# The opening of an encoder layer on one core: modulation columns on VectorE, low weight parts by DMA, x on two queues

## The chip, the core and the metric

The kernel runs as one program on one core of a Trainium2 chip. The core has five engines with an instruction queue each: TensorE (PE, matrix products; its weight loads are listed apart as PEld), VectorE (DVE), ScalarE (ACT), GpSimd (POOL) and SyncE (SP), which here only issues transfers. An engine works through its queue in order, and an instruction that has to wait holds up those behind it. Transfers between main memory and the on-chip memory are issued from SP's, ACT's or POOL's queue and are carried by 16 DMA engines that all queues share. The metric is the device time of one execution in microseconds.

## The reference

One encoder layer on a sequence of 512 tokens with 1024 channels, batch 1, all in float32. A conditioning vector c gives nine modulation vectors of 1024 numbers: shift, scale and gate for each of three sub-layers. The sub-layers are a SwiGLU feed-forward network, a mixer of two kinds of attention, and a second SwiGLU network.

```python
c_act = jax.nn.silu(c)
mod = c_act @ w_mod[l] + b_mod[l]
(sh1, sc1, g1, sh2, sc2, g2, sh3, sc3, g3) = jnp.split(mod, N_MOD, axis=-1)
h = modulate(rmsnorm(x, norm_ffn1[l]), sh1, sc1)          # h * (1 + scale) + shift
x = x + 0.5 * g1[:, None, :] * swiglu(h, w_ffn1_in[l], w_ffn1_out[l])
```

The change is about the first two and the fourth of these lines and about the first products of the fifth. What follows (the mixer, the second network) is not touched.

## The kernel before

**Layout.** Everything is kept transposed: channels lie on the 128 partitions, in eight chunks (`NC` = 8) of 128 channels, and the 512 tokens lie along the free axis. A column is 128 numbers, one per partition: for one modulation vector there are eight columns, one for each chunk. `par` holds small parameters as columns: the three norm gains, the 72 bias columns of `b_mod`, and one more.

**Split products.** A float32 product is made of three products in a faster format: a tensor is split into a high part (a rounding copy) and a low part (what the rounding left), and high times high, high times low and low times high are added up. `split_from` (lines 158 to 160) does that with a copy on ScalarE (line 159) and a subtraction on VectorE (line 160). `load_main`, used later in the kernel, does it in another way (lines 601 to 603): ScalarE writes the high part and also its negative, and a transfer from POOL's queue adds the weights from main memory onto the negative, which leaves the low part.

**A modulation column.** `mod_load` asks for a 128 x 1024 block of `w_mod` on SP's queue (line 196). `mod_col` multiplies it by the broadcast Silu of c (`cact`) and sums each row in one instruction on VectorE (line 206), then adds the bias and puts in the rest with one or two instructions on a single column (lines 213 to 219). For the shift columns of the opening GpSimd makes the product (line 453) and ScalarE the row sum (line 204).

**The opening** (lines 431 to 485). The order of TensorE, VectorE and ScalarE is written out by hand there. SP and GpSimd are ordered by a planner that goes by modelled times, as all engines are in most of the kernel's stages unless a `manual_schedule` block names them.

1. c is broadcast over the partitions by TensorE (line 434). x comes in eight transfers on SP's queue, with `par` after the second (lines 189 and 191).
2. ScalarE squares each chunk of x (line 438), VectorE adds the squares up (line 440), TensorE sums them over the partitions (line 277), VectorE adds the epsilon (line 247), GpSimd takes the power -1/2 (line 248). VectorE puts the result on a diagonal (line 256), and TensorE spreads it over all partitions (line 269).
3. For each chunk k, `hidden` makes the modulated, normalised input: VectorE scales x (line 286, here called the scale step), ScalarE adds the shift and rounds (line 287), VectorE takes the low part (line 289).
4. The first three pairs of column blocks of the network's input weights are multiplied chunk by chunk (line 482): six accumulators, three products each, so 18 products per chunk, with h of that chunk and the block `w1s[k]` of 128 x 768 weights (loaded on line 450, split by `first_split`).

The columns and weights for chunk k + 1 are made while TensorE works on chunk k. The six accumulators take six of the eight banks of the product memory.

**After the opening** `ffn` goes through the other pairs, eight chunks each. After each pair `side1` makes about two more modulation columns (56 are left) and, at its first call, asks for three small inputs (`row`, `pos`, `freq`) that are used much later. Tensors of the kind `u4` (six buffers) hold the `w_mod` blocks, `raw` (four) the weights as loaded, `hi` and `lo` (five each) the split weights; a transfer into a buffer waits on its queue until the last reader of the former content is through.

## Time and profile before

| | |
|---|---|
| time, median of 3 runs | 1116.46 us (1116.37 to 1117.34) |
| the profiled execution's own time | 1117.23 us |
| its span in the trace | 1115.4 us |
| TensorE busy | 1086.0 us (97%) |
| VectorE busy | 739.6 us (66%) |
| ScalarE busy | 536.0 us (48%) |
| GpSimd busy | 147.4 us (13%) |
| first product of the opening / first product after it | 23.47 / 64.50 us |

The span runs from the first to the last instruction of the profiled execution; its own time is 1.83 us longer. A row of the timeline gives the start in us, the duration in us, the engine, the line of the kernel, the operation, what it writes and reads with the shapes, the number of instructions merged in the row, and in brackets the idle time before it with what ended it. [...] Rows of the grouped views give total busy us and mean ns of one.

### The profile page before, as it was taken

To read this page: it belongs to the slowest core of one execution; us is meant where nothing else is said; L and a number is where in the kernel's file an instruction comes from. 1 tells how busy PE (TensorE), PEld (TensorE's weight loads), DVE (VectorE), ACT (ScalarE), POOL (GpSimd) and SP (SyncE) were. 2 spreads that over 40 slices of the span, in tenths; PEclk is the share of its full clock that TensorE was granted. 3 is DMA by queue.
4 is the path that set the end of the run, shared out by engine and by line. 5 is a ranking of instruction groups with operands and counts; after the bars stand their busy time and mean duration, and the time that the engine had idled before them with its cause. 6 is when DMAs were issued, how large, how long until landed. Compare 5 with 4: busy or idle time off the path is not lost.

```text
span 1115.4 us, 16981 instructions
## 1 busy us (share of the span) xinstructions
PE 1086.0 (97%) x6540; PEld 950.5 (85%) x6540; DVE 739.6 (66%) x1441; ACT 536.0 (48%) x895; POOL 147.4 (13%) x152
## 2 busy tenths in 40 slices
PE   4899999999999999999999999999999999999998
PEld 2688888888888998876788877979999999999998
DVE  6998456765733450567642678855888777776767
ACT  3453221223223274567765655534766545654553
POOL 3300000000000011430113300101121111111210
PEclk9999999999999999999999999999999999999999
DMA  8797446766434439874468831862488999799874
GB/s 304 239 353 249 137 153 218 249 242 224 156 87 127 161 115 271 189 171 95 105 158 199 228 103 34 308 187 58 95 200 202 222 231 195 182 224 212 188 145 118
DMA packets 63570, 204.54 MB, mean 183 GB/s; under 512 B 7553, under 2 KB 9729, under 8 KB 63490
## 3 DMA queue, kind: packets, MB, share of 16 engines
q1 hardware_dynamic: 45792, 144.73, 37.6%
q0 software_dynamic: 15392, 54.53, 27.1%
q10 hardware_dynamic: 2306, 4.20, 1.0%
q8 instruction: 51, 0.84, 0.3%
q14 instruction: 29, 0.24, 0.1%
HBM read 194.52 MB, written 8.91 MB: 182 GB/s over the span
## 4 chain that ended last, share of the span: by engine, by line
PE 78%; issue 9%; DVE 5%; DMA 3%; ACT 2%; POOL 1%; SPq 0%; DVEq 0%; POOLq 0%; ACTq 0%
PE sc L154 9%; PE sc L156 9%; PE sc L155 9%; PE acc L154 7%; PE acc L155 6%; PE acc L156 6%; PE sc L1098 3%; PE sc L1100 3%; PE sc L1099 3%; PE acc L1099 3%; PE acc L1100 3%; PE acc L1098 3%; PE acc L656 2%; PE acc L657 2%; PE acc L658 2%
## 5 line engine op out<-in xcount | busy, mean ns | idle before, releaser
L159 ACT CAST hi<-raw 128x1024 fp32r<-128x1024 f32 (+2 forms) x160 | 155.3, 975 | 218.5 <-PE sc L155 130.9
L160 DVE TENSOR_TENSOR lo<-raw,hi 128x1024 fp32r<-128x1024 f32 (+2 forms) x160 | 179.9, 1129 | 60.6 <-ACT hi L159 58.4
L154 PE MATMUL sc<-b,hi 128*128 128x512 f32 (+1 forms) x430 | 159.9, 372 | 0.4 <-ACT b L159 0.4
L155 PE MATMUL sc<-b,hi 128*128 128x512 f32 (+1 forms) x430 | 159.3, 371 | 0.0
L156 PE MATMUL sc<-b,lo 128*128 128x512 f32 (+1 forms) x430 | 159.2, 370 | 0.0
L154 PE MATMUL acc<-b,hi 128*128 128x512 f32 (+1 forms) x352 | 134.1, 381 | 0.0
L155 PE MATMUL acc<-b,hi 128*128 128x512 f32 (+1 forms) x352 | 130.8, 372 | 0.0
L156 PE MATMUL acc<-b,lo 128*128 128x512 f32 (+1 forms) x352 | 130.7, 371 | 0.0
L1098 PE MATMUL acc<-b,hi 128*128 128x256 f32 x374 | 106.2, 284 | 0.1
L1099 PE MATMUL acc<-b,hi 128*128 128x256 f32 x374 | 105.9, 283 | 0.1
L1100 PE MATMUL acc<-b,lo 128*128 128x256 f32 x374 | 105.9, 283 | 0.0
L1100 PE MATMUL sc<-b,lo 128*128 128x256 f32 x358 | 101.4, 283 | 0.0
L1098 PE MATMUL sc<-b,hi 128*128 128x256 f32 x358 | 101.3, 283 | 0.0
L1099 PE MATMUL sc<-b,hi 128*128 128x256 f32 x358 | 101.3, 283 | 0.0
L154 PEld LDWEIGHTS sc<-b,hi 128*128 128x128 f32 x430 | 81.0, 188 | 14.7 <-ACT b L159 0.9
L155 PEld LDWEIGHTS sc<-b,hi 128*128 128x128 f32 x430 | 81.0, 188 | 14.2 <-DVE b L160 0.3
L156 PEld LDWEIGHTS sc<-b,lo 128*128 128x128 f32 x430 | 81.0, 188 | 13.7
L206 DVE CUSTOM_DVE_ANT_0 u<-u,ka 128x1024 f32<-128x1024 f32 x65 | 82.5, 1281 | 12.9 <-DMA u<-w_mod 12.8
L159 ACT CAST hi<-u 128x1024 fp32r<-128x1024 f32 (+1 forms) x51 | 52.2, 1024 | 69.1 <-PE acc L1099 14.1
L160 DVE TENSOR_TENSOR lo<-u,hi 128x1024 fp32r<-128x1024 f32 (+1 forms) x51 | 60.8, 1192 | 28.8 <-ACT hi L159 28.4
L154 PEld LDWEIGHTS acc<-b,hi 128*128 128x128 f32 x352 | 66.4, 189 | 13.7 <-issue 3.5
L156 PEld LDWEIGHTS acc<-b,lo 128*128 128x128 f32 x352 | 66.3, 188 | 11.3
(339 smaller groups left out, 2461.1 us busy)
## 6 DMA issues: line engine op xcount, KB each, us to landing
u<-w_mod SPq DMA_DIRECT2D x72, 512.0 KB, 5.3
raw<-w1i SPq DMA_DIRECT2D x38, 512.0 KB, 4.3
u<-w2i POOLq DMA_DIRECT2D x31, 512.0 KB, 6.1
raw<-w2i SPq DMA_DIRECT2D x31, 512.0 KB, 4.4
raw<-w_gate SPq DMA_DIRECT2D x16, 512.0 KB, 5.1
lo<-w_gate POOLq DMA_DIRECT2D x13, 512.0 KB, 7.3
u<-w2i SPq DMA_DIRECT2D x13, 512.0 KB, 6.9
raw<-w1o SPq DMA_DIRECT2D x16, 384.0 KB, 3.1
```

Source lines behind the costliest of these rows:

```text
L154: PE.matmul(out, wh, xh, start=first, stop=False)
L155: PE.matmul(out, wh, xl, start=False, stop=False)
L156: PE.matmul(out, wl, xh, start=False, stop=last)
L159: S.copy(hi, src)
L160: V.tensor_tensor(lo, src, f(hi), ALU.subtract)
L206: V.tensor_tensor_reduce(out=w, in0=w, in1=cact, scale=1.0, scalar=0.0, op0=ALU.mult, op1=ALU.add, accum_out=t)
L656: PE.matmul(out[t][:, 0:n], hh[k][:, ht], wh[:, o : o + n], start=k == 0, stop=False)
L657: PE.matmul(out[t][:, 0:n], hh[k][:, ht], wl[:, o : o + n], start=False, stop=False)
L658: PE.matmul(out[t][:, 0:n], hl[k][:, ht], wh[:, o : o + n], start=False, stop=k == NC - 1)
L1098: PE.matmul(out, wh[:, s], xh, start=first and j == 0, stop=False, skip_group_check=True)
L1099: PE.matmul(out, wh[:, s], xl, start=False, stop=False, skip_group_check=True)
L1100: PE.matmul(out, wl[:, s], xh, start=False, stop=last and j == 1, skip_group_check=True)
```

## The change

- The columns: the bias, and for gates the factor, is the start value of the reduction, so that a shift or gate column is one instruction. `mod_begin` prepares such start values for all eight columns of a vector at once. A scale column is the reduction and one more instruction. All of them, the shift columns of the opening too, are made on VectorE; GpSimd's product and ScalarE's row sum are gone.
- The weights of the opening: for chunks 1, 3, 5 and 7 the low part is made in `load_main`'s way (two passes on ScalarE and an adding transfer from POOL's queue); for the even ones VectorE subtracts as before, in `first_low`. The high parts are made one chunk earlier than before, and the loads of three chunks are asked for at the start.
- x: chunks 6 and 7 are asked for on POOL's queue, the others on SP's; `par` goes to ACT's queue.
- The norm: the sums are made with `Norm.add` and `close`, in two groups (the sum of seven squares, and the last square). The two Silus of c come after the fourth square.
- TensorE multiplies the identity by itself, 8 + 5 + 4 times, between the steps ahead of the first product.
- The three products of a chunk come in the order high-high, high-low(h), low(weights)-high.
- The order of SP and POOL in the opening is now written out by hand as well.
- The three small inputs are asked for when fewer than 52 columns are left.

```diff
-        nc.sync.dma_start(x[c], a["x"][c])
-        if c == 1:
-            nc.sync.dma_start(par, a["par"])
+        (G if c in BY_POOL else nc.sync).dma_start(x[c], a["x"][c])
...
+    def mod_begin(v):
+        if v in (SH1, SH2, SH3):
+            return par[:, BMOD + v * NC : BMOD + (v + 1) * NC]
...
+        t, begin = modv[v][:, c : c + 1], mod_begin(v)[:, c : c + 1]
+        by = 1.0 if v in norms or v in (SH1, SH2, SH3) else -0.5 if v == G3 and c % 4 < 2 else 0.5
+        V.tensor_tensor_reduce(
+            out=w, in0=w, in1=cact, scale=by, scalar=0.0 if v in norms else begin, op0=ALU.mult, op1=ALU.add,
+            accum_out=t,
+        )
+        if v in norms:
+            V.scalar_tensor_tensor(t, t, par[:, norms[v] + c : norms[v] + c + 1], begin, ALU.mult, ALU.add)
...
-    with tc.manual_schedule(engines={mybir.EngineType.DVE, mybir.EngineType.Activation, mybir.EngineType.PE}):
+    with tc.manual_schedule(engines=BOUND | {mybir.EngineType.SP, mybir.EngineType.Pool}):
...
+        def warm(n):
+            out = bank("sc")[:, 0:P]
+            for i in range(n):
+                PE.matmul(out, ident, ident, start=True, stop=True)
+        warm(8)
+        def first_loads(k):
+            scale = mod_load(SC1, k)
+            raw = sbuf("raw", [P, 1024], F32, RAW)
+            nc.sync.dma_start(raw[:, 0:768], a["w1s"][k])
+            w1[k] = scale, mod_load(SH1, k), raw
+        def first_split(k):
...
+            S.copy(hi, raw)
+            if k in BY_DMA:
+                S.activation(lo, raw, AF.Identity, scale=-1.0)
+                G.dma_start(lo, a["w1s"][k], accum_op=ALU.add)
+        def first_low(k):
+            raw, hi, lo = w1[k][2:]
+            if k not in BY_DMA:
+                V.tensor_tensor(lo, raw[:, 0:768], f(hi), ALU.subtract)
+        for k in range(3):
+            first_loads(k)
+        mod_begin(SC1)
         n1 = Norm()
         for c in range(NC):
+            n1.add(c)
+            if c == 3:
+                for i in range(2):
+                    S.activation(cact[:, i * T : (i + 1) * T], cb[i], AF.Silu)
+        rs = n1.close()
         mod_col(SC1, 0, w1[0][0])
+        warm(5)
+        diag = n1.diagonal(rs)
+        rb1 = n1.spread(diag)
+        warm(4)
         mod_col(SH1, 0, w1[0][1])
+        out1 = [b for _ in range(3) for b in pair_banks()]
         first_split(0)
         for k in range(NC):
             h1 = hidden(rb1, k, SC1, SH1, hh[k], hl[k])
             next(h1)
+            if k + 3 < NC:
+                first_loads(k + 3)
             if k == 0:
+                first_split(1)
+                first_low(0)
+            elif k + 1 < NC:
+                mod_col(SC1, k + 1, w1[k + 1][0])
+            next(h1)
+            if k == 0:
+                mod_col(SC1, 1, w1[1][0])
+            wh, wl = w1.pop(k)[3:]
+            for w, h in ((wh, hh[k]), (wh, hl[k]), (wl, hh[k])):
...
             if k + 1 < NC:
+                mod_col(SH1, k + 1, w1[k + 1][1])
+                first_low(k + 1)
+            if k + 2 < NC:
+                first_split(k + 2)
...
-        while small_loads:
+        credit[0] += n
+        while small_loads and len(rest) < 52:
             nc.sync.dma_start(*small_loads.pop())
-        credit[0] += n
```

More of the change, by code (lines that the diff above doesn't have):

```diff
@@ L435, in layer @@
+        for k in range(3):
+            first_loads(k)
+        mod_begin(SC1)
         n1 = Norm()
         for c in range(NC):
-            sq = f2()
-            S.activation(sq, x[c], AF.Square)
-            if c:
-                V.tensor_tensor(sq, sq, before, ALU.add)
-            before = sq
-        n1.sums(sq, FULL[0], True, True)
-        for i in range(2):
-            S.activation(cact[:, i * T : (i + 1) * T], cb[i], AF.Silu)
-        w1 = {}
-        def first_loads(k):
-            w1[k] = [mod_load(v, k) for v in ((SH1, SC1) if k else (SC1, SH1))]
-            raw = sbuf("raw", [P, 1024], F32, RAW)
-            nc.sync.dma_start(raw[:, 0:768], a["w1s"][k])
-            w1[k].append(raw)
-            if k:
-                G.tensor_tensor(w1[k][0], w1[k][0], cact, ALU.mult)
-                mod_col(SC1, k, w1[k][1])
@@ L470, in layer @@
             next(h1)
+            if k + 3 < NC:
+                first_loads(k + 3)
             if k == 0:
[L472 to L479 removed]
+                first_split(1)
[7 more added lines that the diff above has]
+            for w, h in ((wh, hh[k]), (wh, hl[k]), (wl, hh[k])):
                 for i, out in enumerate(out1):
[L481 to L482 removed]
+                    first, last = k == 0 and w is wh and h is hh[k], k == NC - 1 and w is wl
+                    PE.matmul(out, w[:, i * P : (i + 1) * P], h, start=first, stop=last)
             if k + 1 < NC:
[L484 to L485 removed]
+                mod_col(SH1, k + 1, w1[k + 1][1])
+                first_low(k + 1)
+            if k + 2 < NC:
+                first_split(k + 2)
     rest = [(v, c) for v in (G1, SC2, SH2, G2, SC3, SH3, G3) for c in range(NC)]
```

59 lines of the change are left out of this document (21 added, 38 removed).

## The prediction

> **What bounds the kernel now.** I read the head of the page first, then the busy time by stages (columns: stretch, its length, busy time of PE, PEld, DVE, ACT and POOL, granted clock, DMA share, GB/s).
>
> ```profile
> span 1115.4 us, 16981 instructions
> 24.00:65.00 41.00, 36.86 (x147) 27.47 (x146) 39.56 (x65) 20.16 (x33) 10.64 (x5) 1.00 0.74 255
> 65.00:200.00 135.00, 135.00 (x597) 111.84 (x596) 89.41 (x157) 38.44 (x51) 0.00 (x0) 1.00 0.62 213
> ```
>
> From 65 us on TensorE has no idle time (135.00 of 135), so what ends before 65 us shifts the rest. In the opening the full engine is VectorE: 39.56 of 41 us. Next the timeline of TensorE: the first row is the first product of the opening, then come the first products of chunks 6 and 7 and the first one after the opening.
>
> ```profile
> 23.47 0.80 PE L482 MATMUL acc<-b,hi 128*128 128x512 f32 x1 [3.56 <-ACT b L287]
> 56.17 0.44 PE L482 MATMUL acc<-b,hi 128*128 128x512 f32 x1
> 60.31 0.48 PE L482 MATMUL acc<-b,hi 128*128 128x512 f32 x1
> 64.50 0.39 PE L154 MATMUL acc<-b,hi 128*128 128x512 f32 x1
> ```
>
> The opening's products run from 23.47 to 64.50 us. A chunk with nothing missing takes 60.31 - 56.17 = 4.14 or 64.50 - 60.31 = 4.19, so 4.15 us for 18 products. Eight would be 33.2 us; they take 41.0. The timeline of VectorE, with GpSimd's row beside it, shows chunk 4, one period of it:
>
> ```profile
> 38.67 0.74 DVE L286 SCALAR_TENSOR_TENSOR f<-x,mod,op 128x512 f32<-128x512 f32 x1
> 39.33 1.22 DVE L206 CUSTOM_DVE_ANT_0 u<-u,ka 128x1024 f32<-128x1024 f32 x1
> 40.47 0.08 DVE L206 DVE_READ_ACCUMULATOR2_ANT mod<- 128x1 f32 x1
> 40.53 2.40 POOL L453 TENSOR_TENSOR u<-u,ka 128x1024 f32<-128x1024 f32 x1 [4.91 <-DMA u<-w_mod]
> 40.59 0.22 DVE L213 TENSOR_SCALAR mod<-mod,par 128x1 f32<-128x1 f32 x1
> 40.84 2.10 DVE L214 TENSOR_TENSOR mod<-mod,par 128x1 f32<-128x1 f32 x1
> 42.86 0.74 DVE L289 SCALAR_TENSOR_TENSOR b<-f,mod,b 128x512 fp32r<-128x512 f32 x1
> 43.53 0.15 DVE L216 TENSOR_TENSOR mod<-mod,par 128x1 f32<-128x1 f32 x1
> 43.60 0.95 DVE L160 TENSOR_TENSOR lo<-raw,hi 128x768 fp32r<-128x768 f32 x1
> 44.46 0.73 DVE L286 SCALAR_TENSOR_TENSOR f<-x,mod,op 128x512 f32<-128x512 f32 x1
> ```
>
> From scale step to scale step 44.46 - 38.67 = 5.79 us, of which a one-column multiply takes 2.10: it ends at 42.94, just as GpSimd's two-input multiply does (40.53 + 2.40 = 42.93). VectorE is held while GpSimd multiplies. The same holds in the head, where the chain to the first product reads:
>
> ```profile
> 2.94 3.75 PE L434 MATMUL sc<-u,ones 1*128 1x512 f32 x4 [2.94 <-DMA u<-c]
> 8.57 1.97 ACT L438 ACTIVATE f<-x 128x512 f32<-128x512 f32 x3 [0.29 <-DMA x<-x]
> 10.45 1.06 ACT L444 ACTIVATE ka<-sc 128x512 f32<-128x512 f32 x2
> 5.26 0.68 DVE L440 TENSOR_TENSOR f<-f,f 128x512 f32<-128x512 f32 x1
> 11.68 1.87 PE L277 MATMUL tp<-ones,f 128*128 128x2 f32 x8 [4.99 <-DVE f L440]
> 13.59 0.16 DVE L247 TENSOR_SCALAR sm<-tp 128x4 f32<-128x4 f32 x1 [0.37 <-PE tp L277]
> 13.84 1.03 POOL L248 TENSOR_TENSOR sm<-sm,half 128x4 f32<-128x4 f32 x1 [12.52 <-DVE sm L247]
> 14.90 2.34 POOL L453 TENSOR_TENSOR u<-u,ka 128x1024 f32<-128x1024 f32 x1
> 14.90 2.88 DVE L256 TENSOR_TENSOR f<-ident,sm 128x512 f32<-128x512 f32 x1 [1.15 <-POOL sm L248]
> 17.84 2.08 PE L269 MATMUL op<-f,ones 128*128 128x512 f32 x2 [4.29 <-DVE f L256]
> 18.96 2.17 DVE L216 TENSOR_TENSOR mod<-mod,par 128x1 f32<-128x1 f32 x1
> 21.92 0.74 DVE L286 SCALAR_TENSOR_TENSOR f<-x,mod,op 128x512 f32<-128x512 f32 x1
> ```
>
> The diagonal (2.88) sits under such a multiply too, and a one-column add takes 2.17 where chunk 4's takes 0.15. I call the start of the first scale step t0 (21.92 here); the first product follows 23.47 - 21.92 = 1.55 us later.
>
> **The change, the loop.** GpSimd's seven multiplies and ScalarE's row sums go; VectorE does the shift columns itself. Its price by the period above, start to start: scale step 39.33 - 38.67 = 0.66. A column with its reduction 40.47 - 39.33 = 1.14, as a shift column now ends, so 1.15. A scale column needs the total back and one more small step: 40.59 - 39.33 = 1.26 to the first small step and about 0.11 for it, 1.37; today it is two steps. The low part of h 43.53 - 42.86 = 0.67, taken as 0.66. The low part of a weight chunk 44.46 - 43.60 = 0.86, taken as 0.87, now for even chunks only. A start value read from a column in the reduction is in no row; I take 0 and allow 0.1 us each, 1.6 in all; a gain is excluded, since nothing is taken out of the reduction.
>
> So a chunk with no low part next costs 0.66 + 1.37 + 0.66 + 1.15 = 3.84, with one 4.71. Chunks 0, 1, 3, 5 carry one: the scale steps start at t0 + 0, 4.71, 9.42, 13.26, 17.97, 21.81, 26.52, 30.36. A chunk's products start 1.55 later or 4.15 after the former chunk's: t0 + 1.55, 6.26, 10.97, 15.12, 19.52, 23.67, 28.07, 32.22. The opening ends at t0 + 36.4. TensorE alone would give 1.55 + 33.2 = 34.8: the two engines are nearly level, so either alone can lose 1.5 us unseen. The low part of h now comes behind the scale column, at 0.66 + 1.37 + 0.74 + 0.1 = 2.87 after the scale step; its products are second now, 1.55 + 6 x 0.23 = 2.93 after it: just covered.
>
> ScalarE in its longest chunk has one high part of h and two passes over a weight chunk, about 0.72 + 2 x 0.82 = 2.4 of 4.3 us, and waits there for a weight chunk loaded three chunks ahead. Behind that wait stands the next high part of h, for which TensorE waits; the loads are asked for as their buffers are given back, over two periods (8.6 us) ahead of use, against these times to landing (queue rows of the DMA view, the last line for the accumulating loads; then the rates by queue and one stretch of the head):
>
> ```profile
> raw<-w1s SPq DMA_DIRECT2D x8, 384.0 KB, 5.9
> lo<-w_gate POOLq DMA_DIRECT2D x13, 512.0 KB, 7.3
> DMA to landing us min/median/max: 5.4/7.5/13.1
> q1 hardware_dynamic: 45792, 144.73, 37.6%
> q0 software_dynamic: 15392, 54.53, 27.1%
> 18.00:20.00 2.00, 1.91 (x2) 0.34 (x2) 1.97 (x3) 0.00 (x0) 1.64 (x1) 1.00 1.03 406
> L159 ACT CAST hi<-raw 128x768 fp32r<-128x768 f32 x8 | 6.6, 820 | 2.0 <-DMA raw<-w1s 2.0
> ```
>
> The four low parts by DMA bring 4 x 0.39 = 1.6 MB more, at 27.1/54.53 against 37.6/144.73 per MB, 1.9 times the engine time. Per chunk that is 1.44 + 0.20 x 1.9 = 1.8 MB in 4.35 us, 415 GB/s against the 406 the head reaches: level, and the three chunks loaded ahead are the reserve. I count nothing for it and up to 3 us in the range. Low part of chunk 1: ScalarE is through at t0 + 1.5 + 2 x 0.8 = 3.1; used at 6.26 + 12 x 0.23 = 9.0. Landing in 5.4 gives 8.5, in 7.5 gives 10.6, in 13.1 gives 16.2. For three quarters of the bytes I take 6.5, between the first two: 0.6 us late, which the gap ahead of chunk 2 (10.41 to 10.97) hides. Chunks 3, 5, 7 are split one and a half chunks ahead and have 11 us.
>
> **The head.** Fewer bytes are not asked for and the same 16 DMA engines carry them, so I leave the last x where it is; two queues may bring it 1 us sooner or later. ScalarE's eight squares and two Silus end at 10.45 + 1.06 = 11.51; now a square is last. The sums become two groups, the first behind the sixth add (0.68 after the seventh square), both from 11.6 on. Their cold price is the row of 1.87, their warm price this one:
>
> ```profile
> 385.29 0.95 PE L277 MATMUL tp<-ones,f 128*128 128x2 f32 x8
> 398.14 0.59 PE L269 MATMUL op<-f,ones 128*128 128x256 f32 x2
> ```
>
> Warm: 11.6 + 2 x 0.95 = 13.5; mean 13.7; power 13.8 to 14.85 beside the scale column (13.75 to 15.1), for which I add 0.2; diagonal 15.4 to 16.1 with nothing on GpSimd (0.74, as other steps of 512 columns); spread about 1.0 (from 0.59 for half the columns) to 17.2; the shift column lies beside it. t0 = 17.3. Cold: 0.92 more for each group and 1.1 for the spread, t0 = 20.2. The 17 warming products stand ahead of these on TensorE: 34 instructions at 0.23 (1.87/8, the nearest row) to 1.04 (2.08/2) us; with 128 columns I take 0.23. The first eight (3.7 us) fit between the broadcast of c, over at 6.69, and 11.6; five (2.3) between the sums and the diagonal's end; four (1.8) about fill the 1.55 before the first product.
>
> I take warm, as the row of 385 us is after dense work and TensorE is now at work from 2.9 to about 10.4. [...]
>
> Moved small loads: three issues leave SP's queue between first-FFN weight loads and return after some pairs, where TensorE has no idle time; nothing either way. The small bias steps dropped in the first FFN lie on a VectorE busy 89.41 of 135 us: nothing. After the opening VectorE still owes two low parts of the next weights, 1.2 each; its last h step is done at t0 + 32.6, so they are done at 35, before 36.4.
>
> **Sum.** End of the opening 17.3 + 36.4 = 53.7 for 64.50: 10.8 us. Profiled execution 1117.23, its span 1115.4; 1117.23 - 10.8 = 1106.4. The median of the runs is 0.77 lower than that execution, so 1105.7.
>
> **Rivals.** (a) Low parts late: with 13.1 us to landing chunk 1 waits 7.2, ends at t0 + 17.6, and six chunks at 4.15 end at 42.5, 6.1 later: 1111.8. For: VectorE and the loads are at their fullest there. Against: no wait of the loop before is on the DMA share, which falls to 0.74.
> (b) The cold clock: t0 = 20.2; the first chunk's slow products mostly vanish in VectorE's lead: 1108.6.
> (c) GpSimd's accumulating loads are held back by VectorE, the mirror of what the rows show. From what point slower: chunk 7's low part is asked for at about t0 + 25 = 42.3 and must land after 63 us, 21 us, against 13.1 at most; at 24 us it would be 1119.7. Its issues took 0.86 to 0.92 us where VectorE was full for 85%:
>
> ```profile
> L603 POOL DMA_DIRECT2D lo<-w_gate x13: 865/883/922, 456.4 to 607.1; - x13
> 456.00:462.00 6.00, 6.00 (x28) 4.99 (x27) 5.09 (x12) 4.72 (x7) 4.53 (x4) 1.00 0.83 189
> ```
>
> That speaks against it. [...]
> (d) The gain is given back: at the end of the opening TensorE waits for the next weights or for banks, and the first FFN starts near 64 us all the same: 1116. Against: all of it hangs on releases that come earlier as well.
> (e) x lands earlier and all covers hold: 1103 or less.
>
> **How the numbers follow.** Forecast within 2.2 us of 1105.7: 0.62 (1103.5 to 1107.9). (a), taken as 1109 to 1112: 0.12. (b): 0.10. (c) as far as slower: 0.05, and another 0.02 for the reduction's start value or the wait behind ScalarE growing past 11 us. (d): 0.04. (e): 0.05. The range 1102.8 to 1111.0 takes in forecast, (b), most of (e) and of (a). A measurement of this kernel tells about 0.2%, 2.2 us, from no change: faster 0.89, same 0.04, slower 0.07.
>
> **What would show it.** Right: no multiply on GpSimd in the opening; no one-column step of VectorE near 2 us; t0 between 16.5 and 18.5; scale steps 3.84 and 4.71 apart; first product after the opening at 53 to 55 us, and TensorE full from there. Wrong: sums at 1.87 a group (cold); chunk 1's low products waiting for a DMA; waits of ScalarE for weight chunks; reductions longer than 1.22; products of the first FFN with idle time before them.

## The result and the profile after

The changed kernel takes 1120.02 us (median of 7 runs, 1119.06 to 1121.14) against 1117.30 us for the kernel before on the same chip (7 runs, 1116.37 to 1118.13): ratio 1.0027, interval 1.0015 to 1.0039. It is 0.27% slower. The forecast was 1105.7 us, and the range ended at 1111.0, so both missed.

Where the time went is read from the start of each stage, which is the start of the first product of the line that opens it (the opening's products; the first network; the mixer; the second network, which reaches to the end of the span).

| us | opening's first product | first network starts | mixer starts | second network starts | span |
|---|---|---|---|---|---|
| before | 23.5 | 64.5 | 411.3 | 771.5 | 1115.4 |
| after | 21.9 | 59.0 | 414.7 | 777.0 | 1117.9 |
| length of the stage, after less before | | -5.5 (all up to here) | +8.9 | +2.1 | -3.0 |

-5.5 + 8.9 + 2.1 - 3.0 = +2.5 us. The opening did get shorter, by half of what was forecast. The first network, in which the change touches only small steps of VectorE and three small transfers, became 8.9 us longer (355.7 for 346.8). That loss is the larger part of the story.

The view of busy time by stretches, of the profile after (columns as in the prediction: PE, PEld, DVE, ACT, POOL, clock, DMA share, GB/s):

```profile
24.00:59.00 35.00, 32.41 (x137) 25.09 (x137) 34.26 (x57) 16.25 (x22) 3.14 (x4) 1.00 1.01 345
65.00:200.00 135.00, 135.00 (x580) 108.75 (x580) 80.50 (x119) 34.35 (x45) 0.00 (x0) 1.00 0.58 202
800.00:1090.00 290.00, 290.00 (x2455) 290.00 (x2455) 226.40 (x332) 167.81 (x253) 51.50 (x59) 1.00 0.85 196
```

The row of 65 to 200 us is to be held against the one of before in the prediction. TensorE is full in both, at the full clock in both, and yet it ends 580 products instead of 597. No wait takes the time: each product is longer. VectorE and ScalarE have less to do than before there (80.50 for 89.41, 34.35 for 38.44). A busy share cannot show this; only the count does.

The length of one pair of column blocks says it more exactly. At the end of each pair ScalarE computes a Silu, and the rows of these in the timeline, first of before, then of after, give the period (a pair is 8 chunks x 2 accumulators x 3 = 48 products of 512 columns):

```profile
232.66 0.60 ACT L381 ACTIVATE f<-acc 128x512 f32<-128x512 f32 x1 [3.89 <-PE acc L156]
243.54 0.60 ACT L381 ACTIVATE f<-acc 128x512 f32<-128x512 f32 x1 [3.89 <-PE acc L156]
```

```profile
232.08 0.60 ACT L392 ACTIVATE f<-acc 128x512 f32<-128x512 f32 x1 [4.04 <-PE acc L158]
243.28 0.60 ACT L392 ACTIVATE f<-acc 128x512 f32<-128x512 f32 x1 [4.04 <-PE acc L158]
```

10.88 us became 11.20: 226.7 ns became 233.3 ns for one product, 2.9% more.

In the second network, whose products have 256 columns, it went the other way, though by less: 2455 products in 290 us after; before, the same stretch has

```profile
800.00:1090.00 290.00, 290.00 (x2421) 290.00 (x2420) 222.19 (x326) 163.94 (x249) 51.09 (x59) 1.00 0.87 196
```

so 119.8 ns for a product became 118.1 (290 / 2421, 290 / 2455).

The opening itself, in the timeline of TensorE after: the first product, the two longest waits of its loop, and the first product of the first network.

```profile
21.86 0.50 PE L513 MATMUL acc<-b,hi 128*128 128x512 f32 x1 [0.19 <-ACT b L298]
30.75 0.50 PE L513 MATMUL acc<-b,lo 128*128 128x512 f32 x1 [1.04 <-DMA lo<-w1s]
50.44 0.50 PE L513 MATMUL acc<-b,hi 128*128 128x512 f32 x1 [1.22 <-ACT b L298]
58.98 0.40 PE L156 MATMUL acc<-b,hi 128*128 128x512 f32 x1
```

And one period of VectorE after, chunk 4 as in the prediction:

```profile
38.62 0.75 DVE L297 SCALAR_TENSOR_TENSOR f<-x,mod,op 128x512 f32<-128x512 f32 x1
39.28 1.22 DVE L225 CUSTOM_DVE_ANT_0 u<-u,ka 128x1024 f32<-128x1024 f32 x1
40.55 0.22 DVE L230 SCALAR_TENSOR_TENSOR mod<-mod,par,begin 128x1 f32<-128x1 f32 x1
40.69 0.74 DVE L300 SCALAR_TENSOR_TENSOR b<-f,mod,b 128x512 fp32r<-128x512 f32 x1
41.35 1.28 DVE L225 CUSTOM_DVE_ANT_0 u<-u,ka,par 128x1024 f32<-128x1024 f32 x1
42.55 0.74 DVE L297 SCALAR_TENSOR_TENSOR f<-x,mod,op 128x512 f32<-128x512 f32 x1
```

No small step takes 2 us any more (0.22 instead of 2.10), and the period of a chunk without a low part is 42.55 - 38.62 = 3.93 where 3.84 was forecast. Prices are read from start to start here as well: the row of the scale step says 0.75 us, the next step starts 39.28 - 38.62 = 0.66 after it.

### The profile page after: what moved, and what is told of

It reads as the page before. It is cut to its first block, busy times and chain, and to the rows that moved or that the text cites. A ratio compares the mean times of both kernels' runs of the same rounds, so it can differ in the third digit from the quotient of the medians.

```text
span 1117.9 us, 16995 instructions
## 1 busy us (share of the span) xinstructions
PE 1098.6 (98%) x6582; PEld 952.3 (85%) x6582; DVE 725.9 (65%) x1385; ACT 532.0 (48%) x885; POOL 135.1 (12%) x151
## 4 chain that ended last, share of the span: by engine, by line
PE 80%; issue 9%; DVE 3%; DMA 3%; ACT 2%; POOL 1%; SPq 0%; ACTq 0%; POOLq 0%; DVEq 0%
PE sc L156 9%; PE sc L157 9%; PE sc L158 9%; PE acc L156 7%; PE acc L157 7%; PE acc L158 7%; PE sc L1133 3%; PE sc L1131 3%; PE sc L1132 3%; PE acc L1133 2%; PE acc L1132 2%; PE acc L1131 2%; PE acc L690 2%; PE acc L689 2%; PE acc L691 2%
## 5 line engine op out<-in xcount | busy, mean ns | idle before, releaser
L161 ACT CAST hi<-raw 128x1024 fp32r<-128x1024 f32 (+2 forms) x152 | 148.8, 981 | 230.1 <-PE sc L157 140.7
L162 DVE TENSOR_TENSOR lo<-raw,hi 128x1024 fp32r<-128x1024 f32 (+2 forms) x152 | 172.5, 1139 | 65.2 <-ACT hi L161 62.2
L156 PE MATMUL sc<-b,hi 128*128 128x512 f32 (+1 forms) x430 | 161.8, 376 | 0.0
L157 PE MATMUL sc<-b,hi 128*128 128x512 f32 (+1 forms) x430 | 161.4, 375 | 0.0
L156 PE MATMUL acc<-b,hi 128*128 128x512 f32 (+1 forms) x352 | 135.5, 385 | 0.0
L157 PE MATMUL acc<-b,hi 128*128 128x512 f32 (+1 forms) x352 | 132.2, 376 | 0.0
L156 PEld LDWEIGHTS acc<-b,hi 128*128 128x128 f32 x352 | 66.4, 189 | 15.1 <-issue 3.6
L157 PEld LDWEIGHTS acc<-b,hi 128*128 128x128 f32 x352 | 66.1, 188 | 11.3
```

What stands on the lines that cost most here:

```text
L156: PE.matmul(out, wh, xh, start=first, stop=False)
L157: PE.matmul(out, wh, xl, start=False, stop=False)
L161: S.copy(hi, src)
L162: V.tensor_tensor(lo, src, f(hi), ALU.subtract)
```

## The experiments

Two questions stood open: why the products became slower in stages that the change does not touch, and where half of the opening's gain is. Unless said otherwise the ratios are to the kernel before, run beside it on the same chip. Stage times, pairs and starts are read from the one profiled execution of each kernel, the time is the median of its runs.

### Why the products are slower: the place of the weights in memory

**Theory.** The change adds a small tensor, `begin1` (eight columns, 32 bytes on each partition), which is allotted ahead of the split weights. In the built programs the buffers `hi` and `lo` so begin 32 bytes further on, while the moving tensors of the products (h and its like, buffers `b8`) stay where they were. Addresses do not stand in a profile; these are from the programs that are built from the kernels, in bytes from the start of a partition, first buffer of each kind (the others follow at multiples of 4096 and 8192):

```
              b8 (moving)   hi (weights)   hi - b8, modulo 2048
before          51808         182880           0
after           51808         182912          32
```

The theory is that the pace of the products hangs on the distance between the two. Rivals: the address of the weights by itself (after: a multiple of 64; before: not), or something in the changed program that has nothing to do with memory, such as the small steps of VectorE or the loads.

**The kernel before, weights 32 bytes up.**

```diff
+    def pad(nm):
+        t = keep([P, 8], nm)
+        G.memset(t, 0.0)
...
         def first_split(k):
+            if k == 0:
+                pad("pad_hi")
             hi = sbuf("hi", [P, 1024], F32R, HILO)
```

> The kernel before with 32 unused bytes put ahead of the split weight buffers hi and lo, so that these start at 182912 as in the changed kernel instead of 182880; nothing else. Theory A (the start address of the weight buffers sets the pace of the products; the 512-column ones 226.7 ns before, 233.3 after): the first network loses about 8.9 us, the mixer 2.1, the second network gains 3.2, so about 7.8 us slower than before, 1125; a pair of the first network 11.20 us instead of 10.88. Theory B (the loss comes from the changed order, queues or transfers): as before, 1117.3, a pair 10.88 us.

Measured: 1126.99 us against 1117.04, ratio 1.0092 (1.0074 to 1.0110). Eight unused numbers on each partition make the old kernel 0.9% slower. The first network takes 355.8 us for 346.8. In the traces the kernel with the pad is 8.0 us longer, as the theory had it; the medians differ by 10, since two of its four runs took 3 to 4 us more than the profiled one, and no trace shows why.

**The changed kernel, `begin1` out of the way** (a buffer that is there already is used for it, so that the weights are back at 182880).

```diff
-            t = begins[v] = keep([P, NC], f"begin{v}")
+            t = begins[v] = small(NC) if v == SC1 else keep([P, NC], f"begin{v}")
```

> The changed kernel with the start values of the first scale vector in one of the small rotating buffers, so that hi and lo start at 182880 as before the change; same instructions. Theory A: the opening's gain of 5.5 us stays and the pace of before returns: about 1112, a pair 10.88 us. Theory B: as the changed kernel, 1120, a pair 11.20 us.

Measured: 1111.50 us against 1117.04, ratio 0.9951 (0.9935 to 0.9968). With this one line changed, the change is a gain. The first network takes 346.8 us, as in the kernel before.

**Everything 32 bytes up, and then the weights another 32.** Both start from the kernel just shown, with `pad` as above. The first puts a pad ahead of `ka`, which lies below the moving tensors and the weights: both move by 32, their distance is 0 again, and the weights lie at 182912, just where they lie in the slow kernel. The second adds a second pad ahead of `hi`: distance 32 again, at other addresses.

```diff
+    pad("pad_ka")
     cact = sbuf("ka", [P, D], F32, 1)
```

```diff
+            if k == 0:
+                pad("pad_hi")
             hi = sbuf("hi", [P, 1024], F32R, HILO)[:, 0:768]
```

> As the run with the start values in a small buffer, with 32 unused bytes ahead of all of ka, b8, raw, f2, hi and lo: the moving tensors (b8) start at a multiple of 64 bytes and so do the weights (182912); the distance between both is that of before. Theory A1 (the weights' own address counts, multiples of 64 bytes are slow): pair 11.20 us, about 1120. Theory A2 (the distance between weights and moving tensor counts): pair 10.88 us, about 1112. Theory B: 1120.

> As the former with another 32 bytes ahead of hi and lo: moving tensors at a multiple of 64 bytes, weights 32 bytes past one (182944), distance as in the changed kernel. Theory A1 (the weights' own address): pair 10.88 us, about 1112. Theory A2 (distance): 11.20 us, about 1120. Theory A3 (the moving tensor's own address): a pace of its own. Theory B: 1120.

Measured: 1111.52 us, 0.9953 (0.9938 to 0.9968) for the first; 1121.42 us, 1.0040 (1.0025 to 1.0055) for both pads. In the first all weights lie at the addresses of the slow kernel and the products are at the old pace; in the second they are slow again. So it is neither the address of the weights by itself nor the order or the steps of the program: it is the distance between the weights and what moved with the first pad. That these are the moving tensors is argued, not shown. The programs rule out `f2`, the buffers of intermediate results, which keep their place in the kernel before with a pad and move with the weights in the changed kernel, both slow; `ka` and `raw` moved with the moving tensors in every run, but no product of the first network reads them. The rows of 65 to 200 us, in this order: the kernel before with a pad, the changed one with `begin1` away, all up by 32, and distance 32 again.

```profile
65.00:200.00 135.00, 135.00 (x581) 108.66 (x580) 87.93 (x156) 38.00 (x51) 0.00 (x0) 1.00 0.60 208
```

```profile
65.00:200.00 135.00, 135.00 (x598) 111.77 (x597) 84.52 (x125) 35.54 (x46) 0.00 (x0) 1.00 0.61 210
```

```profile
65.00:200.00 135.00, 135.00 (x597) 111.84 (x596) 83.28 (x125) 35.55 (x46) 0.00 (x0) 1.00 0.61 209
```

```profile
65.00:200.00 135.00, 135.00 (x580) 108.69 (x579) 80.89 (x120) 33.84 (x45) 0.00 (x0) 1.00 0.59 202
```

The kernel with the pad keeps the old steps of VectorE (87.93 us of work, 156 instructions) and has the slow products; the changed kernels with distance 0 have the new, lighter load and the full pace. TensorE's count follows the distance and nothing else in these rows.

**Other distances.** One run each, to see whether 32 is special or 0 is. The pad ahead of `hi` is 64, 96 or 128 bytes, with `begin1` away:

```diff
+    def pad(nm, n=8):
+        t = keep([P, n], nm)
+        G.memset(t, 0.0)
...
+            if k == 0:
+                pad("pad_hi", 16)        # 24 and 32 in the other two
             hi = sbuf("hi", [P, 1024], F32R, HILO)[:, 0:768]
```

> The changed kernel with the start values in a small buffer and 64 unused bytes ahead of the weight buffers: weights 64 bytes further from the moving tensors than in the kernel before. If the distance counts modulo 64: pair 10.88 us, second network 339.2 us, about 1111.5. If it counts modulo a larger power of two: a pair other than 10.88 us.

> The same with 96 bytes. Modulo 64: as with 32, pair 11.20 us, second network about 336 us, about 1121. Otherwise: another pace.

> The same with 128 bytes. Modulo 64 or 128: pair 10.88 us, second network 339.2 us, about 1111.5. Modulo 256 or more: another pace, so far unknown.

| distance modulo 2048 | one pair (48 products of 512) | first network | second network to the start of its last product | time |
|---|---|---|---|---|
| 0 (`begin1` away) | 10.88 us | 346.8 | 339.5 | 1111.50 (median) |
| 32 (after) | 11.20 | 355.7 | 336.3 | 1120.02 (median) |
| 64 | 11.20 | 354.8 | 330.8 | 1112.81 |
| 96 | 11.24 | 356.6 | 335.5 | 1119.22 |
| 128 | 11.15 | 354.1 | 337.9 | 1120.27 |

For the products of 512 columns only 0 of the five gives the short pair. The weights of a pair are read in blocks of 128 columns, which lie 512 bytes apart, and at distance 0 all 48 products start 226 or 227 ns apart; so multiples of 512 bytes are alike here. At the other distances the gaps between starts vary and repeat: nearly every two products at 32 (232 to 235 ns) and 64 (230 to 236), every seven at 96 (231 to 238) and 128 (228 to 241). Seven fits neither the three products of a split nor the two accumulators, so the extra time does not belong to one kind of product. For the 256-column products of the second network, 0 is the slowest, and 64 the fastest. The row of the second network at distance 64, to be held against the 2421 and 2455 above (TensorE even waits 2 us in it):

```profile
800.00:1090.00 290.00, 287.89 (x2491) 287.30 (x2491) 227.24 (x336) 169.86 (x258) 53.22 (x61) 1.00 0.88 199
```

A kernel with distance 0 in the first network and 64 in the second would have both, but the two share their buffers; it was not tried.

**Only the low weights 32 bytes up.** Based on the kernel with x on one queue (below). Two of three products use `hi`, one uses `lo`. If each product paid for its own two operands, only every third would be longer, and a pair would be 10.88 + 0.32 / 3 = 10.99 us.

```diff
             hi = sbuf("hi", [P, 1024], F32R, HILO)[:, 0:768]
+            if k == 0:
+                pad("pad_lo", 8)
             lo = sbuf("lo", [P, 1024], F32R, LO)[:, 0:768]
```

> The kernel with x on SP's queue, with 32 unused bytes between hi and lo: high weights at the good distance from the moving tensors, low weights 32 bytes off. If each product pays by its own weights: a third of the products are slow, a pair takes 10.88 + 0.32/3 = 10.99 us. If one bad buffer sets the pace of all: 11.20 us. If only the weights loaded beside a running product matter: likewise a third, 10.99 us, but the slow product is another of the three.

Measured (one run): 1119.76 us, against 1109.24 for the kernel it starts from, and a pair of 11.20 us. (2.5 us of the difference lie in the opening, where the low part of chunk 1 came later and TensorE waited 2.57 us for it.) The timeline of TensorE shows it (start and modelled duration; lines 160 and 161 are the products with `hi`, 162 those with `lo`):

```profile
100.14 0.40 PE L160 MATMUL acc<-b,hi 128*128 128x512 f32 x1
100.37 0.40 PE L161 MATMUL acc<-b,hi 128*128 128x512 f32 x1
100.61 0.39 PE L162 MATMUL acc<-b,lo 128*128 128x512 f32 x1
100.83 0.40 PE L160 MATMUL sc<-b,hi 128*128 128x512 f32 x1
```

The starts lie 0.23, 0.24 and 0.22 us apart; in ns, from each start to the next and averaged over some 330 of each kind between 70 and 300 us, it is 232.7 from line 160, 239.3 from line 161 and 228.0 from line 162, together 700.0 as in the slow kernel (3 x 233.3) and not 687 (10.99 us over 16). So moving one of the two kinds costs as much as moving both. The product with the moved weights is the shortest of the three, and the longest is the one just ahead of it, beside which these weights are loaded (in the profile after, the weight load of 0.19 us for line 158 starts at 99.81, with the product of line 157). That speaks for an effect between the products in a row, not inside one product; but no run here looks inside, and what in the memory or in TensorE does it stays open.

### Where the rest of the opening's gain is

The runs from here on have distance 0, so the opening is seen by itself. The changed kernel with `begin1` away starts the first network at 59.9 us (64.5 before).

**The columns alone.** The kernel before, with the shift columns made on VectorE and nothing else of the change: this asks whether GpSimd's multiplies were the hold.

```diff
-                G.tensor_tensor(w1[k][0], w1[k][0], cact, ALU.mult)
...
-                mod_col(SH1, k + 1, w1[k + 1][0], on_pool=True)
+                mod_col(SH1, k + 1, w1[k + 1][0])
```

> The kernel before with one part of the change alone: the shift columns of the opening are reductions on VectorE, GpSimd multiplies and ScalarE row sums are gone; order, loads, low parts and the two small bias steps stay, and the layout. Theory: GpSimd's multiplies held VectorE, so no small step near 2 us is left, t0 falls from 21.9 to about 18, and a chunk takes VectorE about 5.1 us (0.66 + 1.6 + 0.66 + 1.3 + 0.87): the opening ends at about 18 + 36 + 1.55 + 4.15 = 59.5 instead of 64.5, time about 1112. Rival: the 1.15 us more of reduction per chunk eat what the hold cost: 1117.

Measured: 1112.51 us, 0.9954 (0.9936 to 0.9972), the same as the whole change with `begin1` away. The timeline of VectorE, the chunk that starts at 24.03:

```profile
24.03 0.74 DVE L286 SCALAR_TENSOR_TENSOR f<-x,mod,op 128x512 f32<-128x512 f32 x1
24.69 1.22 DVE L206 CUSTOM_DVE_ANT_0 u<-u,ka 128x1024 f32<-128x1024 f32 x1
25.95 0.21 DVE L213 TENSOR_SCALAR mod<-mod,par 128x1 f32<-128x1 f32 x1
26.20 0.16 DVE L214 TENSOR_TENSOR mod<-mod,par 128x1 f32<-128x1 f32 x1
26.27 0.75 DVE L289 SCALAR_TENSOR_TENSOR b<-f,mod,b 128x512 fp32r<-128x512 f32 x1
29.15 0.74 DVE L286 SCALAR_TENSOR_TENSOR f<-x,mod,op 128x512 f32<-128x512 f32 x1
```

VectorE does more work than before in this kernel, and its period falls from 5.79 to 29.15 - 24.03 = 5.12 us, since the one-column step takes 0.16 for 2.10. The reading that GpSimd's multiply holds VectorE is right, and it is most of the gain: 4.6 us of the 5.5. In the traces the rest of the change together adds 60.6 - 59.9 = 0.7 us to it in the opening: from t0 to the first network it is 42.6 us here and 38.6 in the changed kernel with `begin1` away, and the new head takes 3.3 of these 4.0 us back (t0 is 18.02 here and 21.30 there). The profiled run of this kernel, 1114.33 us, is the slowest of its four.

**No warming products.**

```diff
-        warm(8)
...
-        warm(5)
         diag = n1.diagonal(rs)
         rb1 = n1.spread(diag)
-        warm(4)
```

> The changed kernel with the start values in a small buffer, without the 17 products of the identity. If they make the first chunk's products fast: these are about 0.43 us apart for some 3 us (10 products, 2 us) and the first chunk ends 2 us later, of which VectorE's lead hides most: 0 to 2 us slower than 1111.5. If they do nothing: 1111.5, first products 0.23 us apart all the same.

Measured: 1117.25 us, 0.9999 (0.9989 to 1.0009), so 5.8 us more than with them; the first network starts at 63.2 for 59.9 us. Rows of TensorE: two of the first products, then the first products of chunk 6 with the wait ahead of them; after that the same wait in the kernel with the warming products.

```profile
23.26 0.63 PE L510 MATMUL sc<-b,hi 128*128 128x512 f32 x1
23.68 0.63 PE L510 MATMUL acc<-b,hi 128*128 128x512 f32 x1
53.37 0.80 PE L510 MATMUL acc<-b,hi 128*128 128x512 f32 x1 [3.71 <-ACT b L298]
53.96 0.63 PE L510 MATMUL sc<-b,hi 128*128 128x512 f32 x1
54.39 0.63 PE L510 MATMUL acc<-b,hi 128*128 128x512 f32 x1
```

```profile
51.49 0.50 PE L513 MATMUL acc<-b,hi 128*128 128x512 f32 x1 [1.57 <-ACT b L298]
```

The first seven products start 0.43 us apart where the kernel with them has 0.23, which is 1.4 us. But VectorE's lead hides this, as expected: the scale step of chunk 6 comes 48.15 - 21.11 = 27.04 us after t0, and 48.34 - 21.30 = 27.04 with the warming products. All of the 3.3 us comes from there on. The planner chose another order for ScalarE: two copies of later weights and a pass over chunk 7's weights stand ahead of the h of chunk 6, where the other kernel has one copy, and chunk 6's first product starts 1.9 us later. After the wait of 3.71 us its products are slow again (0.43 us apart; the granted clock from 24 to 60 us is 0.95 in the mean, 1.00 with the warming products), so that the rest of the opening takes 9.84 for 8.36 us. Of what is left of the 5.8 us, 1.1 lies beyond the opening in the traces and is not explained, and this kernel's runs spread over 4.3 us. What the warming products are worth by themselves this run thus does not show; up to chunk 6 it is nothing.

**The first weights after the opening in the written order**, so that ScalarE's copy can't stand ahead of the last h:

```diff
+            if k == NC - 1:
+                for i, raw in enumerate(nxt):
+                    hi = sbuf("hi", [P, 1024], F32R, HILO)
+                    lo = sbuf("lo", [P, 1024], F32R, LO)
+                    split_from(hi, lo, raw)
+                    nxt[i] = hi, lo
             wh, wl = w1.pop(k)[3:]
```

> The changed kernel with the start values in a small buffer, and the loads and splits of the first network's next pair put into the written order of the opening, behind the last chunk's h, where the planner had put ScalarE's copy ahead of it (TensorE waited 1.57 us for that h). Theory: the opening ends 1.5 to 2.3 us earlier, 57.6 to 58.4, time 1109 to 1110. Rival: the copies, now later, make the next pair late by as much: 1111.5.

Measured: 1112.21 us, 0.9952 (0.9937 to 0.9967): no gain over 1111.50. The opening ends 1.5 us earlier, and the next wait takes it, at the first product of the first network:

```profile
58.10 0.39 PE L524 MATMUL sc<-b,lo 128*128 128x512 f32 x1
59.51 0.50 PE L156 MATMUL acc<-b,hi 128*128 128x512 f32 x1 [1.02 <-ACT f L392]
```

TensorE waits for the Silu that gives back the product memory (line 392), as rival (d) of the prediction had it, at a price of 1 us and not 10.

**No low parts by DMA** (all by VectorE):

```diff
-BY_POOL, BY_DMA = (6, 7), (1, 3, 5, 7)
+BY_POOL, BY_DMA = (6, 7), ()
```

> The changed kernel with the start values in a small buffer and all low parts of the opening by VectorE. Theory (VectorE is the bound): four more steps of 0.87 and 3.5 us later, less the wait for the low part of chunk 1: about 1114.5. Rival (the transfers are full at the end of the opening, share 0.98): 1.6 MB less bring the next weights earlier, and it is about 1111.5 or less.

Measured: 1114.89 us, 0.9981 (0.9972 to 0.9990). From chunk 1 to chunk 6 the scale steps are 4.80 apart, without the short periods of 3.93 between them, and TensorE waits 0.37 to 0.73 us ahead of the chunks; the first network starts at 62.4 for 59.9 us. The transfers are worth 2.5 us of the opening, and 3.4 in the time.

**x on SP's queue alone** (low parts by DMA again):

```diff
-BY_POOL, BY_DMA = (6, 7), (1, 3, 5, 7)
+BY_POOL, BY_DMA = (), (1, 3, 5, 7)
```

> The changed kernel with the start values in a small buffer and all of x on SP's queue. If the second queue helps: t0 later by up to 1 us, 1112.5. If it only takes its share from the chunks that are needed first (the third chunk of x landed at 6.7 to 7.2 us, 6.3 before): t0 earlier by 0.5 to 1 us, 1110.5 to 1111.

Measured: 1109.24 us, 0.9927 (0.9912 to 0.9943). Rows of ScalarE's squares: with two queues (the changed kernel with `begin1` away), the third chunk; with one, the third chunk in the first row and the fourth in the second.

```profile
6.68 0.63 ACT L240 ACTIVATE f<-x 128x512 f32<-128x512 f32 x1 [1.38 <-DMA x<-x]
```

```profile
5.24 0.63 ACT L240 ACTIVATE f<-x 128x512 f32<-128x512 f32 x1 [0.35 <-DMA x<-x]
6.56 0.63 ACT L240 ACTIVATE f<-x 128x512 f32<-128x512 f32 x1 [0.69 <-DMA x<-x]
```

The chunk that is needed third comes 1.4 us later with two queues. This fits the second reading, that the two chunks on the second queue take their share of the 16 DMA engines from the first ones; that share itself was not measured. With one queue the sums start at 11.05 us, with two at 12.60. The planner's order is another one here too: the copies of the next weights come behind the h of chunk 6 on ScalarE and wait 0.25 us at most, and the scale steps of chunks 6 and 7 are 3.93 apart for 5.65. The first network starts at 57.1 us. The two effects were not taken apart further: t0 is 19.75 for 21.30 in the kernel that this one starts from, so about 1.5 of the 2.8 us are the head's.

**The scale column ahead of the power, then one group of sums.** The first moves the column, on VectorE, out of the time in which GpSimd takes the power; the second makes one group of sums instead of two. The first is based on the kernel just shown, the second on the first.

```diff
-        rs = n1.close()
         mod_col(SC1, 0, w1[0][0])
+        rs = n1.close()
```

```diff
+        V.tensor_tensor(n1.acc, n1.acc, n1.last[0], ALU.add)
+        n1.sums(n1.acc, FULL[0], True, True)
         mod_col(SC1, 0, w1[0][0])
-        rs = n1.close()
+        rs = n1.rstd(FULL[0])
```

> The kernel with x on SP's queue, with the first scale column put ahead of the power instead of beside it. If the column holds the power: 1.95 becomes 1.03 us, t0 from 19.75 to about 18.9, time 0.9 lower than the 1109.24 of the run with x on SP. If the power is long for another reason: 1109.2.

> As that run, and all eight squares added before one group of sums, as in the kernel before. If the second group costs its cold price: 1.7 us less on TensorE, 0.6 more on VectorE, t0 about 17.8, time about 1107.2. If the sums were covered: as the former run, 1108.3.

Measured: 1108.72 us, 0.9930 (0.9913 to 0.9946), and 1108.79 us, 0.9929 (0.9915 to 0.9944). Rows of the kernel that it starts from, the scale column's reduction with the power beside it; then of the first of the two: the sums, the power, the spread and the first scale step.

```profile
14.74 1.22 DVE L225 CUSTOM_DVE_ANT_0 u<-u,ka 128x1024 f32<-128x1024 f32 x1
14.91 1.95 POOL L259 TENSOR_TENSOR sm<-sm,half 128x4 f32<-128x4 f32 x1 [13.60 <-DVE sm L258]
```

```profile
10.53 1.95 PE L288 MATMUL tp<-ones,f 128*128 128x2 f32 x16 [0.29 <-DVE f L246]
12.76 1.04 POOL L259 TENSOR_TENSOR sm<-sm,half 128x4 f32<-128x4 f32 x1 [11.45 <-DVE sm L258]
14.57 2.08 PE L280 MATMUL op<-f,ones 128*128 128x512 f32 x2 [0.68 <-DVE f L267]
16.69 0.75 DVE L297 SCALAR_TENSOR_TENSOR f<-x,mod,op 128x512 f32<-128x512 f32 x1 [0.96 <-PE op L280]
```

The power takes 1.04 us with no reduction beside it and 1.95 with one: VectorE holds GpSimd as GpSimd held VectorE. In the profiled executions t0 comes at 16.69 for 19.75, but the medians of the two kernels differ by 0.5 us only, and three of the four runs of the first lie at 1108.7 to 1108.9; the profiled run (1105.57) is 3 us faster than these, so the 3.1 us of its head are in part luck. 0.9 of them are the power, and 0.5 come from x, which landed earlier. The other 1.6 are the sums: the same 16 products take 1.95 us here and 3.57 in the profile of the kernel it starts from, and the identity products behind them start 0.11 us apart here and 0.21 there. One group of sums instead of two takes 1.05 us and has t0 at 16.76, so it brings nothing. These kernels are some 0.7% faster than the kernel before and 1% faster than the changed one; which of the last three is best the times do not tell.

## Why the prediction was wrong

**The step that failed** is the first one: "From 65 us on TensorE has no idle time (135.00 of 135), so what ends before 65 us shifts the rest". With it goes the one in the part on moved loads, "nothing either way", after the opening. A full engine was taken for one of fixed pace, and the sum put what happens behind 65 us at nothing. The pace was not fixed: the new tensor moved the weights by 32 bytes and made the 512-column products 2.9% longer. The first network lost 8.9 us by it. The mixer lost 2.1 (with distance 0 it gains 0.9) and the second network with the tail regained 3.0; that these too come from the distance follows from the kernels with and without the pad, but the mixer's mixed products were not taken apart. Together this is 8.0 of the 13.3 us between the forecast (10.8 less) and the profiled execution (2.5 more); the other 5.3 are the opening's. No rival held this. (d) gave a time close by (1116), for another cause.

With the weights where they had been, the change gives 1111.50 us: faster, by half of what was forecast. So the part on the opening also has terms that were off.

**Right: GpSimd holds VectorE.** No multiply on GpSimd is left and no small step near 2 us; the kernel with the columns alone (0.16 us for the step of 2.10) shows that moving them to VectorE is worth 0.46% by itself.

**The loop: 36.4 forecast, 38.7 measured** (20.30 to 58.98 us). The period without a low part was to be 3.84 and is 3.93, with one 4.71 and 4.80. The reduction with a start value from a column takes 1.28 for 1.22 us; "I take 0 and allow 0.1 us each" was within its bounds. Over the six chunks up to the scale step at 47.35 all this is 0.5 us. The larger part, 1.75, is chunk 6: 52.94 - 47.35 = 5.59 for 3.84. "After the opening VectorE still owes two low parts of the next weights" was wrong in the word after: the planner put one of them (1.23 us), and ahead of it on ScalarE a copy that waits 2.19 us for its load, in front of the last chunk but one. The timeline of ScalarE after:

```profile
48.72 1.05 ACT L161 CAST hi<-raw 128x1024 fp32r<-128x1024 f32 x1 [2.19 <-DMA raw<-w1i]
49.67 0.72 ACT L298 ACTIVATE b<-f,mod 128x512 fp32r<-128x512 f32 x1
```

The prediction had named this danger, for the copies of chunks in the opening, and counted nothing.

**The head: t0 at 17.3 forecast, 20.30 measured.** Four terms, all on the late side: the sums start at 12.92 for 11.6 (x on two queues: "may bring it 1 us sooner or later", it was later); they take 2.26 for 1.9; the power 1.94 for 1.25, where 0.2 was added for the column beside it and 0.9 was the price; the spread 2.08 for 1.0, the cold price. The steps between them were 0.5 shorter than allowed: 1.3 + 0.4 + 0.7 + 1.1 - 0.5 = 3.0. The "warm" choice thus failed for the spread and in part for the sums, and rival (b) was right about them. For warm stood the rows of 385 and 398 us, amid dense products; that TensorE's work from 2.9 to about 10.4 us is enough for their pace was an estimate, and no run shows it: the spread took the cold price behind 0.66 us of idle time. How far the choice fails varies with no change in the opening: in the six other profiles with the same opening (the kernels of the distances: `begin1` away, all up, distance 32 again, 64, 96 and 128) the sums take 2.36 to 3.58 us and t0 lies between 19.05 and 21.91. The same holds for the first products. Here they are 0.23 apart from the second on, but in nine of the thirteen profiles with the same 17 warming products the first two to six are slow (0.43 apart), so these products did not ensure a fast start.

**Chunk 1's low part** was forecast 0.6 us late and is 1.04 late (30.75). It costs nothing at the end, though not because of the gap ahead of chunk 2: from 30.75 on TensorE does not wait before 50.44, so the gaps of the next chunks are gone, and it is the wait of 1.22 us at chunk 6 that takes the delay up. Rival (a) did not come; but the load is what it was said to be: the DMA share is 1.01 from 24 to 59 us, at 345 GB/s, less than the 406 that the head's rate had promised.

**Rival (c), GpSimd's issues held back by VectorE,** is out: the four adding transfers took 0.87 to 0.94 us to issue beside a VectorE that is busy 34.26 of 35 us. These rows show no delay of the issues by the steps of this opening. That VectorE and GpSimd hold each other's computing steps is shown by the one-column step (2.10 us beside GpSimd's multiply, 0.16 without it) and by the power (1.95 us beside a reduction, 1.04 without one).

## What to carry to other kernels

A full engine has a pace, and the pace can change with where the tensors lie (here from 226.7 to 233.3 ns for a product of 512 columns): count instructions per stretch in a stage that the change does not touch before crediting or blaming the part that it does. When a change adds even a small lasting tensor, look at what it shifts, and keep the distance between weights and moving tensors as it was, or try several distances for each shape of product. A single profile of an opening like this one is no measure of it to better than 1 or 2 us, since t0 moved by 2.9 us between kernels with the same opening. And a step that a planner orders is not "after" anything by itself: what it can put in front of the critical step, with the wait that it brings, belongs in the sum.

## What was not expected of the hardware

**Distance and pace.** With the weights and the moving tensors a multiple of 2048 bytes apart, a product of 512 columns takes 226.7 ns; at 32, 64, 96 and 128 bytes more it takes 233.3, 233.3, 234.3 and 232.4 ns (a pair over 48). Products of 256 columns, in the dense stretch of the second network, take 119.8 ns at 0, 118.1 at 32, and at 64 about 115.6 (287.89 / 2491). Moving only the weights of every third product makes the three together as slow as moving all, and the longest of them is the one ahead of the moved weights. The mechanism is open.

**The clock in the head.** In the kernel with the column ahead of the power, the view by stretches shows the granted clock fall while TensorE is hardly ever idle (the stretches begin with the warming products behind the sums, and with the spread):

```profile
12.50:14.50 2.00, 1.40 (x10) 1.11 (x9) 0.83 (x3) 0.00 (x0) 1.04 (x1) 0.71 1.02 412
14.57:16.65 2.08, 2.08 (x3) 1.05 (x4) 1.15 (x2) 0.00 (x0) 0.00 (x0) 0.50 1.03 414
```

The longest idle time of TensorE from 2.95 us to the spread is 0.68 us, and the clock is at 0.50 there. The durations say the same: 16 products for the sums in 1.95 us and then two for the spread in 2.08, where 0.59 for products of half the columns was the row of later in the kernel. (The clock column is the weaker sign ahead of the first change that it records: it says 1.00 through the whole head also for the kernels whose sums take 3.57 and whose identity products start 0.21 apart.) With the same order of work on TensorE the sums take 1.95, 2.26 and 3.57 us in three kernels (this one, the changed one, and the one with x on one queue), behind 0.29, 2.56 and 0.66 us of idle time; what makes the difference no run shows. Later in the opening some waits cost more than their length: after the one of 3.71 us in the kernel without warming products eight products start slowly (53.37 to 56.84 us); in the run with the low weights moved, with its wait of 2.57 us for low weights, the longest product with low weights in the opening is 0.63 us, where 0.40 is the median; after 2.50 us, with one group of sums, the products are at their pace (0.23 us apart) from the second on. What sets the clock, and whether thin products (128 columns, or two columns for the sums) bear on it, was not measured.
